# An fp32 encoder on one core: buffer rings and product order of the seven-product FFN tiles, a spread permutation, and the sums of the last norm

## The chip, the cores and the metric

The kernel runs on one core of a Trainium2 chip. A time is the device time of one execution in microseconds (us). TensorE is PE here (its weight loads are PEld), VectorE DVE, ScalarE ACT, GpSimd POOL, and SyncE, which only issues DMAs in this kernel, SP. A lower time is better.

## What is computed

The reference is a trunk of two encoder layers on 512 tokens of width 1024, in fp32. Each layer adds a token mixer, a cross-attention into a memory and a SwiGLU feed-forward part (FFN), each behind an RMS norm; a last RMS norm ends it. The change lies in the FFN and in the last norm:

```python
def rms_norm(x, g):
    y = x * lax.rsqrt(jnp.mean(x * x, axis=-1, keepdims=True) + EPS)
    return y * g

def swiglu(h, w_gate_up, w_down):
    g, u = jnp.split(h @ w_gate_up, 2, axis=-1)
    return (jax.nn.silu(g) * u) @ w_down

for i in range(2):
    x = x + mixer(rms_norm(x, g_mix[i]))
    x = x + memory_cross_attention(rms_norm(x, g_xq[i]), rms_norm(mem, g_mem[i]), ...)
    x = x + swiglu(rms_norm(x, g_ffn[i]), w_gate_up[i], w_down[i])   # 1024 -> 2 x 2816 -> 1024
return rms_norm(x, g_final)
```

## The kernel before

**Precision.** Every fp32 operand is split into a high part in PE's fast fp32 format (F32R) and a low part, the rest. A product is then three matmuls: high x high, high x low, low x high.

**FFN** (`ffn`, L1153). A layer has 22 gate/up tiles, each of 128 columns of gate and 128 of up. They come in rounds j = 0..7, 8..15 and 16..21, and behind each round stands a down stage that multiplies what the round made with the down weights and adds it to x. Tiles 0, 1, 20 and 21 are computed whole. The 18 between, j = 2..19, are seven-product tiles (`winograd`, L1122): the tile's product is taken as two by two blocks, and by Strassen's scheme in Winograd's form seven block products do for eight. `product` (L1112) issues one of them, 12 matmuls of 128 x 256 (line L1119), so a tile is 84 matmuls. A tile accumulates in three PSUM banks. The bank called mm takes A11, then A12 on top; S takes S2, then S3 and A22; T takes S1, then S4. `seven_tile` (L1196) and the u additions (L1130, L1135) and copies (L1128, L1132) put the parts together on DVE and ACT. A bank is reused by a tile two later; L1203 is the last to read S.

**Left factors** (`left_factors`, L1070). The 1 MB of weights of a tile arrives as a raw tile (ring of two, loaded by SP at L101 or L98). Three factors are plain blocks (A11, A12, A22, function `loaded`): ACT casts the high part (L1087), ACT writes the negated block, rounded to F32R, into the low half (L1088), and POOL issues a DMA of 256 KB that adds the block from HBM on top (L1089), which leaves the low part. Four factors are computed (S1, S2, S3, S4): DVE makes the sum (`summed`, L1095), ACT casts it (L1080), DVE subtracts (L1081). Each of the seven needs one buffer of 128 x 1024. `tile_of` takes them in turn from two rings of four, tagged wl and wh, in the order A11, S2, S1, A12, S3, S4, A22; seven being odd, a factor's ring changes from tile to tile.

**Order.** A scheduler places every engine's instructions in one order ahead of time, and gives a new tile the buffer of its ring that came free first. On the chip each engine then works through its list in that order and waits where an input or a buffer is missing. POOL's accumulate DMAs stand in POOL's list, raw loads in SP's.

**Permutation** (`by_columns`, L1146). The mixer of layer 1 wants the tokens in another order, so between rounds of layer 0 x is permuted: for each of its eight tiles an ACT copy (L1150) and a DVE copy back (L1151). It is called at j = 20 of layer 0.

**Last norm** (`last_step`, L1293). It works in two halves of 256 tokens, for m = 0..7: `sum_sq` (L138) squares x on ACT (L141) and adds into an accumulator on DVE or POOL (L145). At m = 7 `rstd_of` (L147) adds the last square on DVE (L148), sums over partitions by a matmul with ones (L152), scales (L135) and takes the power -1/2 on POOL (L136); ACT and DVE scale the result (L1315, L1317) and SP writes it (L1318).

Of the kernel before, what the change touches and what calls it, by code (L numbers as in the profile page):

```python
# [31 lines left out]
def trunk_kernel(  # L32
# [30 lines left out]
    def x_bank():  # L63
        return bank_of("X", 1)

    def o_bank():
        return bank_of("O", 1)

    def tmp():
        return pp.tile([P, 512], F32, tag="P", name="P")  # L70

    def small(n=4):
        return sm.tile([P, 8], F32, tag="sm", name="sm")[:, :n]
# [991 lines left out]
        T3, T4 = parts(tb)  # L1065
        return dict(T1=T1, T2=T2, T3=T3, T4=T4)

    turn = [0]

    def left_factors(v, src, room):  # L1070

        def tile_of():
            turn[0] ^= 1
            tag = ("wh", "wl")[turn[0]]
            hl = wp.tile([P, 1024], F32R, tag=tag, name=tag)
            return hl.rearrange("p (e k n) -> p e k n", e=2, k=4)

        def parts(x):
            hl = tile_of()
            nc.scalar.copy(hl[:, 0], x)  # L1080
            nc.vector.tensor_sub(hl[:, 1], x, hl[:, 0].bitcast(F32))  # L1081
            return hl[:, 0], hl[:, 1]

        def loaded(i):

            hl = tile_of()
            nc.scalar.copy(hl[:, 0], v[:, i])  # L1087
            nc.scalar.activation(hl[:, 1], v[:, i], AF.Copy, scale=-1.0)  # L1088
            nc.gpsimd.dma_start(hl[:, 1], src[:, i], accum_op=ALU.add)  # L1089
            return hl[:, 0], hl[:, 1]  # L1090

        def summed(op, x, y):
            t = room.tile([P, S], F32, tag="oT", bufs=8, name="ws")
            t = t.rearrange("p (k n) -> p k n", k=4)
            nc.vector.tensor_tensor(t, x, y, op=op)  # L1095
            return t
        r = {}
        a11, a12, a21, a22 = (v[:, i] for i in range(4))
        s1 = summed(ALU.add, a21, a22)
        r["A11"] = loaded(0)  # L1100
        s2 = summed(ALU.subtract, s1, a11)
        r["S2"] = parts(s2)
        r["S1"] = parts(s1)
        r["A12"] = loaded(1)
        s3 = summed(ALU.subtract, a11, a21)
        r["S3"] = parts(s3)
        s4 = summed(ALU.subtract, a12, s2)
        r["S4"] = parts(s4)
        r["A22"] = loaded(3)
        return r  # L1110

# [10 lines left out]
    def winograd(ph, A, Bs):  # L1122

        ba, bb, bd = (f()[:, :256] for f in (mm_bank, s_bank, t_bank))
        t = ph.tile([P, 4, 256], F32, tag="pth", bufs=2, name="pc")
        pc, u = t[:, 0:2], t[:, 2:4]
        product(ba, A, Bs, "A11", "B11", True)
        nc.scalar.copy(pc[:, 0], ba)  # L1128
        product(bb, A, Bs, "S2", "T2", True)
        nc.vector.tensor_add(u[:, 0], pc[:, 0], bb)  # L1130
        product(bd, A, Bs, "S1", "T1", True)
        nc.scalar.copy(pc[:, 1], bd)  # L1132
        product(ba, A, Bs, "A12", "B21", False)
        product(bb, A, Bs, "S3", "T3", False)
        nc.vector.tensor_add(u[:, 1], pc[:, 0], bb)  # L1135
        product(bd, A, Bs, "S4", "B22", False)
        product(bb, A, Bs, "A22", "T4", False)
        return ba, (u[:, 0], bd), (pc[:, 0], bb), (u[:, 1], pc[:, 1])
# [4 lines left out]
    def columns(t):  # L1143
        return t.rearrange("p (c r) -> p r c", r=8)

    def by_columns(ph):  # L1146

        for f in range(KF):
            t = ph.tile([P, S], F32, tag="oT", bufs=8, name="perm")
            nc.scalar.copy(columns(t), rows(xs[f]))  # L1150
            nc.vector.tensor_copy(xs[f], t)  # L1151

    def ffn(layer, ph, step, normed, fin):  # L1153
        wgu = w_gate_up[layer]
        wd = w_down[layer]
        lo, hi = slice(0, 256), slice(256, 512)
        whole = []

        def blocks(w):
            return w.rearrange("p e (k n) -> p e k n", k=4)  # L1160

        def whole_factors(j):

            v = load(wgu[j], 4, 4 * P).rearrange("p e (k n) -> p (e k) n", k=4)
            return [split(v[:, i * KF:(i + 1) * KF], KF, P) for i in range(2)]

        def factors(j):
            v = blocks(load(wgu[j], 4, 4 * P))
            return left_factors(v, blocks(wgu[j]), ph)

        cross(layer, ph, normed, lambda: whole.append(whole_factors(0)), step[0])
        xh, xl, Bs, rstd = step[1]()
        whole.append(whole_factors(1))
        bc = row_bcast(lambda: ph.tile([P, S], F32, tag="oT", bufs=8, name="bc"), rstd)

        def whole_tile(wg, wu, behind=None, own=0):


            bg, bu = s_bank(), t_bank()
            steps = [(b, w, i) for b, w in ((bg, wg), (bu, wu)) for i in range(KF)]  # L1180

            def issue(part):
                for bank, (wh, wl), i in part:
                    k = i % 2 * 4 + i // 2
                    mm3(bank, wh[:, k], wl[:, k], xh[i], xl[i], i == 0, i == KF - 1)
            if behind is None:
                issue(steps)
            else:
                issue(steps[:own])
                with tc.issue_after(behind):  # L1190
                    issue(steps[own:])
            g = ph.tile([P, S], F32, tag="ptl", bufs=2, name="g")
            nc.vector.tensor_mul(g, bg, bc)
            return g, bu

        def seven_tile(A):  # L1196
            c11, c12, c21, c22 = winograd(ph, A, Bs)
            g = ph.tile([P, 2, S], F32, tag="ptl", bufs=2, name="g")
            g, u = g[:, 0], g[:, 1]
            nc.vector.tensor_mul(g[:, lo], c11, bc[:, lo])  # L1200
            nc.vector.tensor_add(g[:, hi], *c12)
            nc.vector.tensor_mul(g[:, hi], g[:, hi], bc[:, hi])
            nc.vector.tensor_add(u[:, lo], *c21)  # L1203
            nc.vector.tensor_add(u[:, hi], *c22)
            return g, u

        A2 = None
        for f0, f1 in ((0, 8), (8, 16), (16, NF)):
            ah, al = [], []
            for j in range(f0, f1):  # L1210
                if layer == 0 and j == NF - 2:
                    by_columns(ph)
                if j == 0:
                    A2 = factors(2)
                if j < 2:
                    g, u = whole_tile(*whole[j], *((marks["sum"], 12) if j == 0 else (marks["bc"], 4)))
                elif j < NF - 2:
                    g, u = seven_tile(A2 if j == 2 else factors(j))
                else:
                    g, u = whole_tile(*whole_factors(j))  # L1220
                sg = tmp()
                nc.scalar.activation(sg, g, AF.Silu)
                nc.vector.tensor_mul(sg, sg, u)
                h = ph.tile([P, 2, S], F32R, tag="wo", bufs=8, name="act")
                h, l = h[:, 0], h[:, 1]
                nc.scalar.copy(h, sg)
                nc.vector.tensor_sub(l, sg, h.bitcast(F32))
                ah.append(h)
                al.append(l)
            n = f1 - f0  # L1230
            last = f1 == NF

            def down_weights(mp):
                return load(wd[f0 * P:f1 * P, mp * 256:(mp + 1) * 256].rearrange("(k p) n -> p k n", p=P), n, 256)

            if last and layer == 1:
                down_by_halves(down_weights, n, ah, al, bc, fin)
                break
            for mp in range(KF // 2):
                v = down_weights(mp)  # L1240
                for mj in range(2):
                    m = mp * 2 + mj
                    bank = down_bank(m)
                    wh, wl = split(v[:, :, mj * P:(mj + 1) * P], n, P)
                    for k in range(n):
                        mm3(bank, wh[:, k], wl[:, k], ah[k], al[k], k == 0, k == n - 1)
                    t = tmp()
                    if last:
                        nc.vector.tensor_mul(columns(t), rows(bank), rows(bc))
                    else:  # L1250
                        nc.vector.tensor_mul(t, bank, bc)  # L1251
                    (nc.vector if m % 2 or last else nc.gpsimd).tensor_add(xs[m], xs[m], t)  # L1252
                    if last:
                        fin(m)
# [38 lines left out]
    def last_step(ph, m, half):  # L1293
# [2 lines left out]
            nat.append(ph.tile([P, NT // 2, D], F32, tag="qT", bufs=2, name="nat"))  # L1296
            st["acc"] = tmp()[:, :256]
        xm = xs[m][:, half * 256:(half + 1) * 256]
        last = sum_sq(st["acc"], xm, m)
        xg = tmp()[:, :256]  # L1300
        nc.scalar.activation(xg, xm, AF.Copy, scale=gcols[:, 67 + m:68 + m])
        b = (t_bank() if m % 2 else s_bank())[:, :256]
# [2 lines left out]
        nc.vector.tensor_copy(nat[half][:, :, m * P:(m + 1) * P],  # L1305
                              b.rearrange("p (t d) -> p t d", t=2))
        if m == KF - 1:
            rstd = rstd_of(st["acc"], last, nc.vector)
            for t in range(2):
                n = nat[half][:, t]  # L1310
                w = D // 2
# [90 lines left out]
```

## Time and profile before

| | |
|---|---|
| median of three runs | 1389.03 us (1387.33 to 1391.44) |
| the profiled execution | 1391.77 us, span 1390.0 us |
| mean granted clock of PE | 0.993 of full speed |
| PE busy | 1346.9 us (97%) |
| DVE busy | 988.7 us (71%) |
| ACT busy | 791.7 us (57%) |
| POOL busy | 446.8 us (32%) |

The span runs from the first instruction to the last; times in the trace count from its start. An engine's busy time says how much it has to do, not where it holds the others up. For that one looks at what PE waited for, at the chain of work that ended last, and at the windows in which a wait falls. Durations below are those of the one profiled execution, which lies 2.7 us above the median.

### The profile page before, as it was taken

Reading aid. Unit: us, or ns where it says so; the run is one execution under the profiler, and the core shown is the slowest. Engines: PE = TensorE matmul, PEld = TensorE weight load, DVE = VectorE, ACT = ScalarE, POOL = GpSimd, SP = SyncE. Lnnn points to the kernel's source line nnn. Section 1 sums busy time; section 2 is a strip of 40 time slices with the busy share of each in tenths; the row PEclk is TensorE's granted clock in tenths of the full one; section 3 lists DMA queues with packets and bytes.
Section 4 is the critical chain, followed back from the end, with each engine's and each line's share of the span. In section 5 each row is a group of like instructions: output and inputs, shape, how many; then the busy total and the mean of one; then the engine's idle time right before and its main releaser. Section 6 shows DMA issues by size and latency. Waiting matters only on the chain.

```text
span 1390.0 us, 24186 instructions
## 1 busy us (share of the span) xinstructions
PE 1346.9 (97%) x9131; PEld 1231.2 (89%) x9131; DVE 988.7 (71%) x1950; ACT 791.7 (57%) x1601; POOL 446.8 (32%) x575
## 2 busy tenths in 40 slices
PE   8898999999999999999999999999999999999997
PEld 8897889998998998898987888798989989998996
DVE  6988886778865875676579745657697766856765
ACT  5467775656743663473468555655566626743543
POOL 4856445212212220200324546842122112212111
PEclk9999999999999999999999999999999999999999
DMA  7111023312853873553122132134207636754721
GB/s 238 62 61 31 1 92 122 122 62 39 191 151 100 189 186 112 135 145 95 50 71 67 33 91 85 61 110 144 82 9 167 175 106 156 175 140 115 181 69 61
DMA packets 93086, 148.78 MB, mean 107 GB/s; under 512 B 7520, under 2 KB 65835, under 8 KB 87339
## 3 DMA queue, kind: packets, MB, share of 16 engines
q1 hardware_dynamic: 77418, 118.93, 26.6%
q0 software_dynamic: 15552, 28.32, 12.4%
q8 instruction: 72, 1.18, 0.3%
q14 instruction: 44, 0.35, 0.1%
HBM read 145.13 MB, written 2.10 MB: 106 GB/s over the span
## 4 chain that ended last, share of the span: by engine, by line
PE 77%; DVE 8%; DMA 7%; ACT 4%; issue 3%; POOL 1%; SPq 0%; POOLq 0%; ACTq 0%; DVEq 0%
PE mm L129 12%; PE mm L130 12%; PE mm L131 12%; PE S L1119 8%; PE mm L1119 6%; PE T L1119 5%; DMA wl<-in_w_gate_up_dram 3%; PE O L553 2%; PE S L129 2%; PE S L130 2%; PE S L131 2%; PE T L275 2%; PE T L130 1%; PE T L129 1%; PE T L131 1%
## 5 line engine op out<-in xcount | busy, mean ns | idle before, releaser
L117 ACT CAST wh<-raw 128x1024 fp32r<-128x1024 f32 (+4 forms) x132 | 130.3, 991 | 139.4 <-PE mm L130 50.9
L123 DVE TENSOR_TENSOR wl<-raw,wh 128x1024 fp32r<-128x1024 f32 (+3 forms) x114 | 139.1, 1221 | 25.8 <-ACT wh L117 23.7
L256 POOL TENSOR_SCALAR P<-P,sm 128x512 f32<-128x512 f32 (+2 forms) x128 | 80.7, 643 | 82.1 <-DVE sm L254 62.6
L1089 POOL DMA_DIRECT2D wh<-in_w_gate_up_dram x54 | 47.0, 871 | 166.2 <-ACT wh L1088 103.4
L130 PE MATMUL mm<-act,wh 128*128 128x512 f32 (+1 forms) x264 | 98.9, 375 | 0.0
L131 PE MATMUL mm<-act,wl 128*128 128x512 f32 (+1 forms) x264 | 98.7, 375 | 0.0
L129 PE MATMUL mm<-act,wh 128*128 128x512 f32 (+1 forms) x264 | 98.3, 376 | 0.0
L1119 PE MATMUL S<-bf,wl 128*128 128x256 f32 x648 | 87.2, 283 | 1.1 <-DVE pc L1135 1.1
L1119 PE MATMUL S<-bf,wh 128*128 128x256 f32 x648 | 86.2, 283 | 0.0
L1089 POOL DMA_DIRECT2D wl<-in_w_gate_up_dram x54 | 47.3, 876 | 114.1 <-ACT wl L1088 42.8
L1119 PEld LDWEIGHTS S<-bf,wl 128*128 128x128 f32 x648 | 81.8, 192 | 1.5 <-DVE pc L1135 1.5
L1119 PEld LDWEIGHTS S<-bf,wh 128*128 128x128 f32 x648 | 81.9, 192 | 0.5
L1095 DVE TENSOR_TENSOR ws<-raw 128x512 f32<-128x512 f32 x72 | 49.5, 688 | 40.4 <-DMA raw<-in_w_gate_up_dram 40.4
L129 PE MATMUL mm<-wh,xgh 128*128 128x256 f32 (+1 forms) x256 | 74.1, 290 | 3.0 <-ACT rt L418 2.3
L145 POOL TENSOR_TENSOR P<-P 128x512 f32<-128x512 f32 (+1 forms) x21 | 26.4, 1255 | 152.8 <-ACT P L141 152.8
L1252 POOL TENSOR_TENSOR x<-x,P 128x512 f32<-128x512 f32 x16 | 25.2, 1577 | 153.5 <-DVE P L1251 153.5
L1080 ACT CAST wh<-ws 128x512 fp32r<-128x512 f32 x72 | 44.5, 619 | 50.2 <-PE mm L130 17.7
L131 PE MATMUL mm<-wh,xgl 128*128 128x256 f32 (+1 forms) x256 | 73.1, 286 | 0.0
L130 PE MATMUL mm<-wl,xgh 128*128 128x256 f32 (+1 forms) x256 | 73.1, 286 | 0.0
L123 POOL TENSOR_TENSOR wl<-raw,wh 128x256 fp32r<-128x256 f32 x80 | 59.1, 770 | 31.6 <-ACT wh L117 31.6
L279 DVE TENSOR_TENSOR ptl<-T,pth 128x512 fp32r<-128x512 f32 (+2 forms) x96 | 57.6, 616 | 13.3 <-ACT pth L278 13.1
L1087 ACT CAST wh<-raw 128x512 fp32r<-128x512 f32 x54 | 33.6, 621 | 54.7 <-PE mm L130 23.6
(420 smaller groups left out, 4758.4 us busy)
## 6 DMA issues: line engine op xcount, KB each, us to landing
raw<-in_w_gate_up_dram SPq DMA_DIRECT2D x44, 1024.0 KB, 5.5
raw<-in_w_down_dram SPq DMA_DIRECT2D x16, 1024.0 KB, 5.6
wl<-in_w_gate_up_dram POOLq DMA_DIRECT2D x54, 256.0 KB, 5.7
wh<-in_w_gate_up_dram POOLq DMA_DIRECT2D x54, 256.0 KB, 5.7
raw<-in_w_xkv_dram SPq DMA_DIRECT2D x8, 1024.0 KB, 5.2
raw<-in_w_down_dram SPq DMA_DIRECT2D x8, 768.0 KB, 4.9
raw<-in_w_in_ab_dram SPq DMA_DIRECT2D x5, 1024.0 KB, 6.7
raw<-in_w_out_ab_dram SPq DMA_DIRECT2D x4, 1024.0 KB, 5.1
```

Of the source, the lines that this page charges most:

```text
L117: nc.scalar.copy(hv, v)
L123: low.tensor_sub(lv[:, q], v[:, q], hv[:, q].bitcast(F32))
L129: nc.tensor.matmul(o, lh, rh, start=start, stop=False)
L130: nc.tensor.matmul(o, lh, rl, start=False, stop=False)
L131: nc.tensor.matmul(o, ll, rh, start=False, stop=stop)
L256: nc.gpsimd.tensor_scalar(p, p, ri[:, j:j + 1], 1.0, op0=ALU.mult, op1=ALU.mult)
L279: nc.vector.tensor_sub(ptl[:, k0:k1, j * P:(j + 1) * P], tv, hv.bitcast(F32))
L1080: nc.scalar.copy(hl[:, 0], x)
L1087: nc.scalar.copy(hl[:, 0], v[:, i])
L1089: nc.gpsimd.dma_start(hl[:, 1], src[:, i], accum_op=ALU.add)
L1095: nc.vector.tensor_tensor(t, x, y, op=op)
L1119: nc.tensor.matmul(bank, x, y, start=start and k == 0 and i == 0, stop=k == n - 1 and i == 2, skip_group_check=True)
```

## The change

Four edits. First, the rings: a loaded factor always takes a buffer of the ring wl, a computed one always one of wh (three and four a tile). Second, in `winograd` the product S2 is issued ahead of A11. Third, the permutation is called in four pieces of two tiles, at j = 16 to 19. Fourth, in the last norm the squares of m = 6 and m = 7 are not added to the accumulator on DVE or POOL; accumulator and squares go to PE each by itself, as matmuls with ones that add up in PSUM (six of one column in each half, where two were).

```diff
     def left_factors(v, src, room):
-        def tile_of():
-            turn[0] ^= 1
-            tag = ("wh", "wl")[turn[0]]
+        def tile_of(tag):
             hl = wp.tile([P, 1024], F32R, tag=tag, name=tag)
...
         def parts(x):
-            hl = tile_of()
+            hl = tile_of("wh")
...
         def loaded(i):
-            hl = tile_of()
+            hl = tile_of("wl")
...
+        product(bb, A, Bs, "S2", "T2", True)
         product(ba, A, Bs, "A11", "B11", True)
         nc.scalar.copy(pc[:, 0], ba)
-        product(bb, A, Bs, "S2", "T2", True)
...
-    def by_columns(ph):
+    def by_columns(ph, fs):
-        for f in range(KF):
+        for f in fs:
...
-                if layer == 0 and j == NF - 2:
-                    by_columns(ph)
+                if layer == 0 and 16 <= j < 20:
+                    by_columns(ph, (2 * j - 32, 2 * j - 31))
...
-        last = sum_sq(st["acc"], xm, m)
+        if m < KF - 2:
+            sum_sq(st["acc"], xm, m)
+        else:
+            sq = tmp()[:, :256]
+            nc.scalar.activation(sq, xm, AF.Square)
+            if m == KF - 2:
+                st["sums"] = x_bank()[:, 0:1], o_bank()[:, 0:1]
+            for a in (st["acc"], sq) if m == KF - 2 else (sq,):
+                for t in range(2):
+                    nc.tensor.matmul(st["sums"][t], a[:, t * P:(t + 1) * P], ones[:, 0:1],
+                                     start=a is st["acc"], stop=m == KF - 1)
...
-            rstd = rstd_of(st["acc"], last, nc.vector)
+            rstd = small(2)
+            mean = small(2)
+            for t in range(2):
+                nc.vector.tensor_scalar(mean[:, t:t + 1], st["sums"][t], 1.0 / D, EPS, op0=ALU.mult, op1=ALU.add)
+            nc.gpsimd.tensor_tensor(rstd, mean, mhalf[:, :2], op=ALU.pow)
```

In the changed kernel lines have moved up by four in most of the FFN: the matmuls of a product are L1115, the casts and subtractions of computed factors L1076 and L1077, of loaded ones L1083 and L1084, the accumulate L1085, the sums L1091, the u additions L1126 and L1131, the last reader of S L1199, the permutation L1146 and L1147.

**PE, j = 11 to 12 in layer 0.** Before, from S3 of one tile (12 matmuls into S) to the second matmul of the next tile's A11 (bank mm):

```order
L1119 MATMUL S<-bf,wh 128x256 x12
L1119 MATMUL mm<-xgh,wl 128x256
L1119 MATMUL T<-xgh,wl 128x256
L1119 MATMUL T<-xgl,wl 128x256
L1119 MATMUL T<-xgh,wl 128x256 x2
L1119 MATMUL T<-xgl,wl 128x256
L1119 MATMUL T<-xgh,wl 128x256 x2
L1119 MATMUL T<-xgl,wl 128x256
L1119 MATMUL T<-xgh,wl 128x256 x2
L1119 MATMUL T<-xgl,wl 128x256
L1119 MATMUL T<-xgh,wl 128x256
L1119 MATMUL mm<-xgl,wl 128x256
```

With the change, from the same S3 on:

```order
L1115 MATMUL S<-bf,wh 128x256 x14
L1115 MATMUL T<-xgh,wh 128x256
L1115 MATMUL T<-xgl,wh 128x256
L1115 MATMUL T<-xgh,wh 128x256 x2
L1115 MATMUL T<-xgl,wh 128x256
L1115 MATMUL T<-xgh,wh 128x256 x2
L1115 MATMUL T<-xgl,wh 128x256
L1115 MATMUL T<-xgh,wh 128x256 x2
L1115 MATMUL T<-xgl,wh 128x256
L1115 MATMUL T<-xgh,wh 128x256
L1115 MATMUL S<-bf,wh 128x256 x10
L1115 MATMUL mm<-xgh,wl 128x256
```

Before, the first A11 matmul stood ahead of S4 (into T) and the rest right behind it; now two matmuls of S2 stand there (they make 14 of the first row), its other ten behind S4, and A11 after them.

**ACT, the start of round two in layer 0.** The numbers of raw name the tile: 5537 is the round's first seven-product tile (A11 5541, A12 5553, S4 5564 and A22 5567), 5675 its second (A11 5679). Before:

```order
L1080 CAST wh_5564<-ws_5562 128x512
L1080 CAST wl_5559<-ws_5557 128x512
L1087 CAST wh_5679<-raw_5675 128x512
L1088 ACTIVATE wh_5679<-raw_5675 128x512
L1087 CAST wl_5567<-raw_5537 128x512
L1088 ACTIVATE wl_5567<-raw_5537 128x512
L1128 COPY pc_5574<-mm_5571 128x256
```

With the change:

```order
L1083 CAST wl_5567<-raw_5537 128x512
L1084 ACTIVATE wl_5567<-raw_5537 128x512
L1076 CAST wh_5564<-ws_5562 128x512
L1083 CAST wl_5679<-raw_5675 128x512
L1084 ACTIVATE wl_5679<-raw_5675 128x512
L1076 CAST wh_5685<-ws_5683 128x512
L1125 COPY pc_5574<-mm_5571 128x256
```

The first tile's A22 (from raw_5537) stood behind the second tile's A11; now it stands ahead of it, and so does the cast of S4.

**DVE, j = 4 and 5 in layer 0.** g_4709 belongs to the tile j = 3 and its last addition reads the bank S_4618; ws_4999 is the first sum of the tile j = 6 and waits for its raw load. Before:

```order
L1081 TENSOR_TENSOR wl_4869<-ws_4867,wl_4869 128x512
L1130 TENSOR_TENSOR pc_4758<-pc_4758,S_4756 128x256
L1202 TENSOR_TENSOR g_4709<-g_4709,bc_4327 128x256
L1203 TENSOR_TENSOR g_4709<-pc_4620,S_4618 128x256
L1095 TENSOR_TENSOR ws_4999<-raw_4997 128x512
L1223 TENSOR_TENSOR P_4715<-P_4715,g_4709 128x512
L1081 TENSOR_TENSOR wh_4872<-ws_4861,wh_4872 128x512
```

With the change:

```order
L1198 TENSOR_TENSOR g_4709<-g_4709,bc_4327 128x256
L1223 TENSOR_TENSOR act_4580<-P_4577,act_4580 128x512
L1077 TENSOR_TENSOR wh_4748<-ws_4746,wh_4748 128x512
L1077 TENSOR_TENSOR wh_4869<-ws_4867,wh_4869 128x512
L1091 TENSOR_TENSOR ws_4999<-raw_4997 128x512
L1199 TENSOR_TENSOR g_4709<-pc_4620,S_4618 128x256
L1091 TENSOR_TENSOR ws_5005<-ws_4999,raw_4997 128x512
```

The addition that frees the S bank stood ahead of the sum that waits for the load; now it stands right behind it.

## Rows read from the trace of the kernel before

**Rows 1.** The page of the profiled execution, part 1.

```profile
PE 1346.9 (97%) x9131; PEld 1231.2 (89%) x9131; DVE 988.7 (71%) x1950; ACT 791.7 (57%) x1601; POOL 446.8 (32%) x575
```

**Rows 2.** The table by windows, busy us summed over six FFN stretches of 340 us.

```profile
sum 340.00, PE 332.93 PEld 325.39 DVE 261.83 ACT 227.07 POOL 79.19; mean PE 55.49 PEld 54.23 DVE 43.64 ACT 37.85 POOL 13.20
```

**Rows 3.** Waits of PE (total, times, longest): layer 0, layer 1; one on the timeline.

```profile
PE mm L1119 <- ACT pc L1128: 1.2, 1, 1.2
PE S L1119 <- DVE pc L1135: 1.1, 1, 1.1
PE mm L1119 <- DMA wl<-in_w_gate_up_dram: 0.8, 1, 0.8
...
PE mm L1119 <- DMA wl<-in_w_gate_up_dram: 3.0, 4, 1.7
PE mm L1119 <- DMA wh<-in_w_gate_up_dram: 0.8, 2, 0.4
...
1065.48 0.50 PE L1119 MATMUL mm<-xgh,wl 128*128 128x256 f32 x2 [1.70 <-DMA wl<-in_w_gate_up_dram]
```

**Rows 4.** The chain that ended last, from 350 to 583 us: start, length, what.

```profile
350.47 2.89 PE S L1119 x24
...
446.95 7.94 DMA raw<-in_w_gate_up_dram
...
573.16 8.94 DMA raw<-in_w_gate_up_dram
```

**Rows 5.** The timeline of ACT, then of POOL, from 477 to 479 us.

```profile
477.24 0.62 ACT L1087 CAST wl<-raw 128x512 fp32r<-128x512 f32 x1 [0.30 <-PE S L1119]
...
478.69 0.87 POOL L1089 DMA_DIRECT2D wl<-in_w_gate_up_dram  x1 [1.48 <-DVE pc L1130]
```

**Rows 6.** The accumulate line L1089: one alone (503 us), then all of layer 1.

```profile
DMA to landing us min/median/max: 4.0/4.0/4.0
...
DMA to landing us min/median/max: 4.0/5.7/9.0
```

**Rows 7.** The tile of the permutation: its copies on ACT and on DVE.

```profile
L1150 ACT COPY perm<-x x8: 1165/1210/1217, 590.2 to 602.9; 128x512 f32<-128x512 f32 x8
L1151 DVE COPY x<-perm x8: 420/427/428, 593.2 to 604.2; 128x512 f32<-128x512 f32 x8
```

**Rows 8.** Line L1089 at 446, 572, 1152 and 1278 us: one accumulate each.

```profile
DMA to landing us min/median/max: 6.8/6.8/6.8
...
DMA to landing us min/median/max: 6.1/6.1/6.1
...
DMA to landing us min/median/max: 8.0/8.0/8.0
...
DMA to landing us min/median/max: 6.0/6.0/6.0
```

**Rows 9.** A wait of DVE in layer 1 (total, times, longest); then its timeline.

```profile
DVE ws L1095 <- DMA raw<-in_w_gate_up_dram: 21.0, 15, 2.3
...
492.93 0.69 DVE L1095 TENSOR_TENSOR ws<-raw 128x512 f32<-128x512 f32 x1
```

**Rows 10.** The tile of the raw loads: 455-520 us, 1287-1300 us.

```profile
DMA to landing us min/median/max: 5.3/5.6/5.8
...
DMA to landing us min/median/max: 5.2/6.2/7.3
```

**Rows 11.** The timeline of the end; then L152 in the first half.

```profile
1379.85 0.42 ACT L141 ACTIVATE P<-x 128x256 f32<-128x256 f32 x1 [1.39 <-DVE x L1286]
1380.36 0.43 DVE L148 TENSOR_TENSOR P<-P 128x256 f32<-128x256 f32 x1 [0.28 <-ACT P L141]
1380.71 0.44 PE L1304 MATMUL T<-identr,P 128*128 128x128 f32 x2 [1.65 <-ACT P L1301]
1380.88 0.53 PEld L152 LDWEIGHTS X<-ones,P 128*128 128x128 f32 x4
...
L152 PE MATMUL X<-ones,P x4: 169/250/250, 1364.0 to 1364.2; 128*128 128x1 f32 x4
```

More of the change, by code (lines that the diff above doesn't have):

```diff
@@ L1066, in right_factors @@
         return dict(T1=T1, T2=T2, T3=T3, T4=T4)
-    turn = [0]
     def left_factors(v, src, room):
-        def tile_of():
-            turn[0] ^= 1
-            tag = ("wh", "wl")[turn[0]]
+        def tile_of(tag):
             hl = wp.tile([P, 1024], F32R, tag=tag, name=tag)
```

## The prediction

> **What bounds the kernel now.** I read the page first, then the table by windows, then the waits, then the chain and the timeline around each wait. The page [rows 1] is to show that TensorE (PE) is busy in 97% of the span: what the change can give back is PE idle time. The windows [rows 2] are to show how much of it lies in the change's reach: in six stretches of seven-product tiles PE is busy for 332.93 of 340 us and lacks 7.07. DVE is busy for 262 us there, so it has less room than ACT with 227. The waits [rows 3] name nine gaps: seven end with the landing of an accumulate DMA (the low part of an A11 factor), one with L1135 on DVE, one with the ACT copy L1128.
>
> These idle times are too short as they stand. A matmul record lasts 0.283 us, yet the next one starts 0.120 us later (24 in 2.88 us, [rows 4]), so each gap is really 0.16 us longer; and the second matmul after a gap starts 0.10 late as well (two take 0.50, [rows 3], not 0.28 + 0.12). The nine waits sum to 6.9 us, and 9 x 0.26 makes it 9.25. At five more places the gap is too small for the view; from the starts of the matmuls I estimate 1.25 us there. Together **10.5 us**: A11 waits 7.4, two waits behind a raw load 1.6, the permutation 1.4.
>
> How each arises. A11: after the last matmul that reads a ring buffer, ACT casts and negates and POOL issues; 477.24 to 478.69 is 1.45 us [rows 5], and with the handover 1.61 from the release. The DMA then lands after 4.0 us at best, 5.7 in the median and up to 9.0 [rows 6], so release to landing is 5.6 to 10.6. Today A11 at most tiles takes a buffer that was freed 55 to 64 matmuls of 0.12 us (6.6 to 7.7 us) before its low part is read. Raw: DVE stands in order; the sum L1095 waits for a 1 MB load of 7.94 or 8.94 us, [rows 4], and L1135, on which PE depends, stands behind it. Permutation: eight ACT copies of 1.21 us at 590 to 603 us [rows 7], and L1128 at 607.7 is behind them.
>
> **The change part by part.**
>
> *Rings.* The same 18 x 3 accumulates and 18 x 4 computed factors run in each layer: nothing is added on any engine. What moves is which buffer each takes, and by the order on PE I counted the matmuls from release to low read. For A11 it becomes 60 to 74 (7.2 to 8.9 us) at most tiles, the product order included. A12 has 98 or more, A22 114 or more. The A22 of a round's first tile finds its buffer free some 6 us earlier, and ACT, and POOL's queue after it, take that A22 ahead of the second tile's A11 instead of behind it. SP's queue keeps its order, and the raw load that waits there for this A22's casts goes earlier too; with that the two waits of L1135 go (-1.6). **But at the second tile of rounds two and three of each layer it falls**, from 9.1 us to 52 matmuls, 6.24 us: there PE still starts A11 ahead of S2, and ACT does S4's cast ahead of A11's. The time needed is 1.61 + 0.52 for that cast, plus the DMA. That DMA is not in the trace, so I bound it: from below by the lone one, 4.0 us [rows 6] (wait 0), from above by the same four tiles today, whose DMAs run beside raw loads and took 6.8, 6.1, 8.0 and 6.0 us [rows 8]: 1.61 + those, less 6.24, makes 2.2 + 1.5 + 3.4 + 1.4 = 8.4 us for the four. Since A22's DMA, which today runs beside it, will be out of the way by some 6 us, I take the low end, 4.0 to 4.7 us: 0.4 a tile, **1.6 us**.
>
> The row says that a lone 256 KB accumulate takes 4.0 us [rows 6]. The Trainium skill, page "DMA: Bandwidth & Descriptors", section "Anatomy of one DMA — SWDGE (gpsimd) path", fits a GpSimd-issued DMA as 2.0 us plus bytes over 436 GB/s, an estimated 2.6 us here. By that figure the four tiles would not wait at all and the sum would be 1.6 us lower; the trace speaks against it, and I use the row.
>
> *S2 first.* S2 needs no DMA, only cast and subtraction, and its T2 right factor is ready. What it needs sooner is the S bank and its two sums: S2 now starts 1.8 us after A22 of two tiles before ends at the least, where it was 3.0. In that time DVE must do L1203, which frees the bank (an addition of that size takes 0.43, [rows 11]). At ten tiles that row now stands behind the s1 sum of the next raw load, or the u0 addition does. Walking the order with 0.69 us a sum [rows 9] and a raw load of 5.5 us, the bank is free 0.68 us early at six tiles, the addition 0.95 early at four. Raw loads in mid-stage took 5.3 to 5.8, in the third round up to 7.3 [rows 10], so a few of them run over by some tenths: I put **0.7 us** between 0 and the second rival's price.
>
> *The other A11s.* 7.2 to 8.9 us against a chain of 1.61 + 5.7 in the median [rows 6]: some still run late. Bounds are 0 and today's 7.4; with a tile's three DMAs now spread over one ring I take **0.7**.
>
> *Permutation.* Four of the ACT copies go into the down stage ahead of round three, four into its first tiles. The same 8 x 1.21 us of ACT and 8 x 0.43 of DVE run where PE has weights ready and no pc copy stands behind; -1.4. If this cover were missing, the wait would come back at most once, 1.4.
> Today's DVE copies at 593 to 604 run beside accumulates, and no PE wait in [rows 3] ends with one of those DMAs. The Trainium skill, page "SBUF — State Buffer", section "SBUF: two separate sides", holds that an fp32 SBUF copy on DVE keeps GpSimd from writing descriptors. By it the four copies beside the first tile's DMAs would cost at most 4 x 0.43 = 1.7 us; the rows show no such wait, and I take nothing.
>
> *Tail.* After the last Square (ends 1380.27) DVE's L148 took 0.43 and with its handover held PE until 1380.88 [rows 11]. Now two small matmuls follow the Square: -0.6; the second tensor_scalar gives 0.15 back: -0.45. The extra matmuls are four per half, two passes each, a pass 0.08 us [rows 11] to 0.12 us [rows 4] after the last; I take 0.11. In the second half PE idles for 1.65 us there [rows 11] and they are covered; in the first half PE is the bound, +0.9. Net **+0.45**, between -0.45 and +0.9.
>
> *Sum*: -10.5 + 1.6 + 0.7 + 0.7 + 0.45 = -7.05. The profiled execution took 1391.8 us, 2.7 above the median of the runs; its waits are taken as those of any run, so the median becomes 1389.0 - 7.05 = **1382.0 us**.
>
> **The rivals.**
> *(a) At four tiles the change does not do what it says*: A11 still comes first there, with the shortest distance of all, and its DMA stays as slow as today: +8.4 instead of 1.6, sum -0.25, 1388.8 us. For it: rows 8 are measured there. Against: A22's DMA moves away.
> *(b) DVE's order* (slower): at ten tiles the S bank or u0 waits behind a sum that waits for a raw load. If raw loads took 7.9 us as at 446.95 [rows 4], six waits of 1.7 and four of 1.5 cost 16.2 us where I put 0.7: 1382.0 + 15.5 = 1397.5. The gain is used up from a load of 7.1 us on. For it: DVE already waits 21.0 us for raw loads in one FFN [rows 9]. Against: mid-stage loads stay at 5.3 to 5.8 [rows 10].
> *(c) The DMAs crowd*: three accumulates through one ring come at other moments, and the A11 waits stay at 7.4 (for 1.6 + 0.7): 1387.1 us.
>
> **How the numbers follow.** My forecast has 0.70, each rival 0.10. About 0.3%, 4.2 us, is what a measurement can tell from no change: 1384.8 and 1393.2 are the marks. My own range is 1378 (every rest at zero) to 1386; a tenth of its 0.70 lies above 1384.8, and a fifth of (a) and (c) stops short of their price and stays faster: 0.63 + 0.04 = 0.67. Slower is (b) less its mild end, 0.08. The rest, 0.25, is within 0.3%. The range runs from 1378.5 to 1389.0, which takes in (a) and (c) and leaves out (b).
>
> **What would show it.** Right: on the timeline of the changed kernel no wait of L1115 for wl at third and later tiles of a round; short ones at the second tiles of rounds two and three; none for a pc copy near 607. L1091's waits for raw stay near 20 us a layer and none of PE's waits ends with L1199 or L1126. Wrong: PE waits of over 1 us for wl at the four second tiles (a), for DVE's L1199 or L1126 with a raw load ahead (b), or for wl spread over all tiles (c). In the tail the first L1317 should start some 0.5 us after the last Square's matmuls begin, with no DVE addition between.

## The result

The change is slower: 1398.19 us in the median (1395.15 to 1401.62, five runs) beside 1389.03 us, a ratio of 1.0062 (95% interval 1.0046 to 1.0079). The forecast was 1382.0 us; the second rival, DVE's order, had 1397.5.

The page of the changed kernel, its first lines. PE has 6 us more of busy time than in [rows 1] and the span is 9.8 us longer.

```profile
span 1399.8 us, 24105 instructions
...
PE 1353.0 (97%) x9147; PEld 1239.8 (89%) x9147; DVE 982.8 (70%) x1950; ACT 792.7 (57%) x1601; POOL 444.6 (32%) x573
```

The waits of PE in the changed kernel (total, times, longest), first in the FFN of layer 0, then of layer 1. These are all that the view has for the seven-product matmuls, L1115.

```profile
PE S L1115 <- DVE g L1199: 5.9, 3, 2.5
...
PE S L1115 <- DVE g L1199: 8.1, 3, 3.1
```

Of the nine waits of [rows 3] none is left: no A11, no pc copy, no u1. In their place stand six, all for L1199, the addition that frees the S bank, and together they are 14.0 us long where the nine had 6.9. The wait of the raw sums, which [rows 9] gave with 21.0 us in layer 1, has grown to 33.1 us:

```profile
DVE ws L1091 <- DMA raw<-in_w_gate_up_dram: 33.1, 16, 4.7
```

One of the six, on the timeline of the changed kernel: POOL's accumulates (A11, A12, A22 of one tile), SP's raw load, then DVE, then PE.

```profile
483.56 0.86 POOL L1085 DMA_DIRECT2D wl<-in_w_gate_up_dram  x1 [3.60 <-ACT wl L1084]
485.21 0.86 POOL L1085 DMA_DIRECT2D wl<-in_w_gate_up_dram  x1 [0.79 <-ACT pc L1128]
487.61 0.86 POOL L1085 DMA_DIRECT2D wl<-in_w_gate_up_dram  x1 [1.54 <-PE S L1115]
...
487.34 0.33 SPq L101 DMA_DIRECT2D raw<-in_w_gate_up_dram  x1
...
496.45 0.69 DVE L1091 TENSOR_TENSOR ws<-raw 128x512 f32<-128x512 f32 x1 [4.21 <-DMA raw<-in_w_gate_up_dram]
497.06 0.41 DVE L1199 TENSOR_TENSOR g<-pc,S 128x256 f32<-128x256 f32 x1
...
497.53 0.80 PE L1115 MATMUL S<-bf,wh 128*128 128x256 f32 x2 [2.53 <-DVE g L1199]
```

The three accumulates are issued within 4.1 us, and the raw load goes out 2.1 us behind the second of them and 0.3 us ahead of the third. It lands 9.1 us later, at 496.4. DVE's list has the first sum of that load (L1091) ahead of L1199, so L1199 starts at 497.06, though the A22 matmuls that it reads had ended over 4 us before; PE, which needs the bank for S2, stands for 2.53 us. One tile earlier DVE has the same two instructions in the same order, but the load, issued at 478.82, took 5.3 us, and PE did not wait:

```profile
DMA to landing us min/median/max: 5.3/5.3/5.3
...
484.14 0.69 DVE L1091 TENSOR_TENSOR ws<-raw 128x512 f32<-128x512 f32 x1 [0.94 <-DMA raw<-in_w_gate_up_dram]
484.75 0.41 DVE L1199 TENSOR_TENSOR g<-pc,S 128x256 f32<-128x256 f32 x1
```

In the whole kernel the first sum of a raw load stands directly ahead of L1199 at ten of the 36 tiles. At six of them the load took 7.9 to 9.7 us, and these are the six waits; at the other four it took 5.3 to 5.5 us, and PE had none.

In the kernel before, at the tile of the 2.53 us wait, POOL's and SP's timeline read:

```profile
481.92 0.86 POOL L1089 DMA_DIRECT2D wh<-in_w_gate_up_dram  x1 [2.36 <-ACT wh L1088]
486.06 0.86 POOL L1089 DMA_DIRECT2D wl<-in_w_gate_up_dram  x1 [3.28 <-ACT wl L1088]
...
485.79 0.33 SPq L101 DMA_DIRECT2D raw<-in_w_gate_up_dram  x1
```

There A12 went out 3.9 us ahead of the load, A22 0.3 us behind it, and the load took 5.3 us. Over the second rounds of the two layers (455 to 520 us, 1160 to 1225 us) the raw loads of the changed kernel landed after

```profile
DMA to landing us min/median/max: 5.3/6.9/9.2
...
DMA to landing us min/median/max: 5.3/7.2/9.7
```

where the kernel before had 5.6 in the median and at most 5.8 us from 455 to 520 [rows 10], and 5.6 and 7.6 from 1160 to 1225. Loads of down weights that start in these windows are among them.

Behind a wait PE is slow as well. The table by windows around 497 us: window, its length, busy us of the engines, then PEclk, the clock that was granted.

```profile
core 0: us, PE busy (x) PEld busy (x) DVE busy (x) ACT busy (x) POOL busy (x), PEclk, DMA share, GB/s
492.70:494.70 2.00, 2.00 (x19) 2.00 (x18) 0.00 (x0) 2.00 (x5) 0.73 (x1) 1.00 0.63 157
494.70:497.50 2.80, 0.30 (x3) 0.10 (x1) 1.05 (x3) 1.06 (x3) 0.99 (x2) 0.94 0.68 117
497.50:500.00 2.50, 2.47 (x11) 2.47 (x12) 2.50 (x5) 0.62 (x1) 0.00 (x0) 0.50 0.68 116
500.00:502.00 2.00, 2.00 (x17) 2.00 (x16) 2.00 (x4) 0.62 (x1) 0.00 (x0) 0.85 0.01 1
502.00:504.00 2.00, 2.00 (x19) 2.00 (x18) 0.60 (x3) 1.31 (x3) 0.51 (x1) 1.00 0.03 8
```

The granted clock falls to 0.50, the lower of its two levels (1.2 GHz), when PE starts again after the wait, and is back at 1.00 by 502 us; 11 matmuls ran in 2.5 us where 19 run in 2.0. It fell so behind four of the six waits (those of 2.02, 2.53, 3.10 and 2.34 us), not behind the other two (1.35 and 2.63 us). Between the starts of one seven-product matmul and the next, what goes beyond the usual 0.12 us adds up to 21.3 us in the changed kernel, 15.4 us of it at the waits and 5.9 us elsewhere, nearly all of that matmuls at the slow clock, and to 10.6 us in the kernel before. The difference, 10.7 us, is close to what the profiled executions differ by (9.85 us; the medians by 9.2).

The other two edits did what they were to do. The permutation's copies now run between 550 and 588 us, and PE has no wait for a pc copy:

```profile
L1146 ACT COPY perm<-x x8: 1140/1180/1206, 550.1 to 587.4; 128x512 f32<-128x512 f32 x8
```

In the last norm, on the timeline of the end, the last Square, the first sum, the first tensor_scalar, the power and the scaling:

```profile
1390.26 0.42 ACT L1299 ACTIVATE P<-x 128x256 f32<-128x256 f32 x1 [1.39 <-DVE x L1282]
1390.73 0.38 PE L1304 MATMUL X<-ones,P 128*128 128x1 f32 x2 [0.40 <-ACT P L1299]
1391.15 0.16 DVE L1317 TENSOR_SCALAR sm<-X 128x1 f32<-128x1 f32 x1 [0.36 <-PE X L1304]
1391.61 0.71 POOL L1318 TENSOR_TENSOR sm<-sm,mhalf 128x2 f32<-128x2 f32 x1 [7.30 <-DVE sm L1317]
1392.35 1.33 ACT L1325 ACTIVATE nat<-nat,sm 128x512 f32<-128x512 f32 x2 [1.27 <-POOL sm L1318]
```

From the start of the last Square to the first sum it is 0.47 us, where [rows 11] had 1.03 (1379.85 to 1380.88). From the last matmul of the last down stage to the end of the span it is 11.08 us, where it was 11.66. But the stretch ahead of that, from the last 512-column matmul, which stands ahead of both halves of the last down stage, has grown from 38.20 to 38.77 us; PE does six of the one-column matmuls for the first half in it, where it did two. Together it is 49.85 us in both kernels.

### The profile page after: what moved, and what is told of

The parts are those of the page before. It is cut to its first block, busy times and chain, and to the rows that moved or that the text cites. A ratio compares the mean times of both kernels' runs of the same rounds, so it can differ in the third digit from the quotient of the medians.

```text
span 1399.8 us, 24105 instructions
## 1 busy us (share of the span) xinstructions
PE 1353.0 (97%) x9147; PEld 1239.8 (89%) x9147; DVE 982.8 (70%) x1950; ACT 792.7 (57%) x1601; POOL 444.6 (32%) x573
## 4 chain that ended last, share of the span: by engine, by line
PE 83%; DVE 6%; DMA 5%; ACT 3%; issue 2%; POOL 0%; SPq 0%; POOLq 0%; ACTq 0%; DVEq 0%
PE mm L129 12%; PE mm L130 12%; PE mm L131 12%; PE S L1115 10%; PE mm L1115 7%; PE T L1115 6%; DMA raw<-in_w_gate_up_dram 4%; PE O L553 3%; PE S L129 2%; PE S L130 2%; PE S L131 2%; PE T L275 2%; PE T L130 1%; PE T L131 1%; PE T L129 1%
## 5 line engine op out<-in xcount | busy, mean ns | idle before, releaser
L1085 POOL DMA_DIRECT2D wl<-in_w_gate_up_dram x108 | 94.0, 870 | 280.6 <-ACT wl L1084 154.7
L1076 ACT CAST wh<-ws 128x512 fp32r<-128x512 f32 x144 | 87.8, 621 | 97.4 <-PE S L1115 31.2
L1115 PE MATMUL S<-bf,wh 128*128 128x256 f32 x864 | 122.0, 291 | 14.0 <-DVE g L1199 14.0
L1115 PEld LDWEIGHTS S<-bf,wh 128*128 128x128 f32 x864 | 113.9, 198 | 15.6 <-DVE g L1199 15.2
L1115 PE MATMUL mm<-xgh,wl 128*128 128x256 f32 x576 | 118.0, 286 | 0.0
L1077 DVE TENSOR_TENSOR wh<-ws,wh 128x512 fp32r<-128x512 f32 x144 | 97.9, 685 | 0.7
L1115 PEld LDWEIGHTS mm<-xgh,wl 128*128 128x128 f32 x576 | 96.3, 195 | 0.2 <-DMA wl<-in_w_gate_up_dram 0.2
L1091 DVE TENSOR_TENSOR ws<-raw 128x512 f32<-128x512 f32 x72 | 49.5, 688 | 60.9 <-DMA raw<-in_w_gate_up_dram 60.9
L1115 PE MATMUL mm<-xgl,wl 128*128 128x256 f32 x288 | 82.0, 285 | 0.0
L1083 ACT CAST wl<-raw 128x512 fp32r<-128x512 f32 x108 | 66.8, 619 | 23.0 <-PE mm L1115 16.6
```

The source lines that it names most:

```text
L1115: nc.tensor.matmul(bank, x, y, start=start and k == 0 and i == 0, stop=k == n - 1 and i == 2, skip_group_check=True)
```

## The experiments

Three theories stood against each other. **R**: the ring split brings three accumulates and a raw load together, the load becomes long, and DVE's order hands this on to the S bank. **S**: S2 first costs by itself, since it needs the bank sooner. **C**: the clock fell, for whatever reason, and that is the loss. All kernels of a group ran on one chip with the kernel before; each interval is that of the ratio to it.

### One part alone, one part undone

The ring split alone (A11 first, permutation and last norm as before):

```diff
-        def tile_of():
+        def tile_of(tag):
...
-            hl = tile_of()
+            hl = tile_of("wh")
...
-            hl = tile_of()
+            hl = tile_of("wl")
```

> The kernel before with the ring split alone (loaded factors in wl, computed ones in wh; A11 still the first product, permutation and last norm as before). Three theories. R: the ring split lets the three accumulates of every second tile start within 4 us, beside one raw load, which then takes 8 to 9.7 us instead of 5.5, and it places the first sum of that load on DVE ahead of the addition that frees the S bank. S: S2 first is what costs, because it needs the S bank 1.4 us sooner, whatever the rings. C: PE's granted clock fell (0.988 in the changed kernel), and that is the loss. Here R expects raw loads of 8 us and more again where accumulates bunch, and PE waits for DVE of 5 to 15 us in all behind the raw sum, by the order's slack of 0.7 to 1.5 us at some 20 tiles: 1388 to 1400 us. S expects no wait for the S bank and the A11 waits reduced: 1383 to 1387. C makes no difference between the edits and expects the clock to tell: 1395 or more with a clock of 0.99 or less.

Measured: 1386.99 us beside 1387.55, ratio 0.9993 (0.9982 to 1.0004). Waits of PE for L1199, layer 0 and layer 1:

```profile
PE S L1115 <- DVE g L1199: 2.0, 2, 1.4
...
PE S L1115 <- DVE g L1199: 1.5, 1, 1.5
```

So the bank waits come with A11 first too, three of them and 3.5 us, less than R's 5 to 15, and A11 waits of 1.9 us are left; the split gains nothing that can be told from zero. The time lies just under R's range and in that of S, but S expected no such wait. Theory C's 1395 us did not come. The ring split also sets DVE's order: in the traces the first sum of a raw load stands at most three instructions ahead of the addition that frees the S bank at 18 of the 36 tiles here and at 12 in the change, and at none in the kernel before and in the runs with the rings in turn.

S2 first alone, rings in turn:

```diff
+        product(bb, A, Bs, "S2", "T2", True)
         product(ba, A, Bs, "A11", "B11", True)
         nc.scalar.copy(pc[:, 0], ba)
-        product(bb, A, Bs, "S2", "T2", True)
```

> The kernel before with S2 issued ahead of A11 alone; rings in turn as before. R expects raw loads of 5.2 to 6.5 us in the middle of the rounds, no PE wait for the addition that frees the S bank, and A11 waits only at the second tiles of rounds two and three (A11 has 8.8 to 11.2 us elsewhere, 6.5 there): some 2 us left of 7.4, so 1382 to 1385 us. S expects the six waits of 1.5 to 3.3 us for the S bank as in the change, 1393 to 1397. C expects no gain unless the clock rises.

Measured: 1393.69 us, ratio 1.0039 (1.0025 to 1.0053). The time lies in S's range, but none of S's waits came: there is no wait for the S bank. The raw loads are as R said (the second rounds, as above), and R's time is missed:

```profile
DMA to landing us min/median/max: 5.7/5.9/6.2
...
DMA to landing us min/median/max: 5.6/5.8/5.9
```

A11 waits are left, 6.7 us in all (layer 0, layer 1), and the longest, four of 1.2 to 2.8 us by the matmuls' starts (452, 581, 1157 and 1283 us), are at the second tiles of rounds two and three:

```profile
PE mm L1119 <- DMA wh<-in_w_gate_up_dram: 4.1, 3, 2.6
...
PE mm L1119 <- DMA wh<-in_w_gate_up_dram: 2.6, 3, 1.3
```

That is my rival (a): A11 is early and close behind its buffer's release at just these four tiles, and its DMA runs beside a raw load. In the change, with the rings split, it did not come. Three waits of 1.9 us in all for ACT's cast L1080, which the kernel before does not have, and the permutation's wait stand beside these.

The change without its ring split was slower than the kernel before too:

```diff
-        def tile_of(tag):
+        def tile_of():
+            turn[0] ^= 1
+            tag = ("wh", "wl")[turn[0]]
```

> The change with its ring split undone (S2 first, permutation spread and sums on PE stay). R expects what S2 first alone gives, with the permutation's wait of 1.4 us gone and 0.5 us more on the path in the last norm: 1381 to 1384 us, and no wait of L1128 behind the permutation. S expects the change's time, 1396 to 1399.

Measured: 1392.35 us, ratio 1.0032 (1.0016 to 1.0048); A11 waits of 3.5 and 3.0 us in the two layers, none behind the permutation, none for the S bank. Its twelve executions lie in two bunches, six of 1388.3 to 1390.6 us and six of 1394.1 to 1396.7; the profile is one of the lower, and what parts them no run shows. R's number is missed, by the profile for the same reason as in the run before; S is out, for S2 first stands here without its waits.

The permutation and the last norm alone (the change with its ring split undone, as above, and A11 as the first product again):

> The kernel before with the spread permutation and the last norm's sums on PE alone; rings in turn, A11 first. My terms were -1.4 for the permutation and +0.45 for the last norm: 1386 to 1389 us, no wait of L1119 for a pc copy near 607 us, the A11 and raw waits as before (9 us in all), and in the tail no DVE addition ahead of the sums. If the permutation's copies on DVE delay the accumulates that run beside them, an A11 wait near 575 to 600 us grows by up to 1.7 us instead.

Measured: 1389.16 us beside 1389.67, ratio 0.9997 (0.9984 to 1.001). No wait behind the permutation is left; the A11 and raw waits are 7.5 us in the view of this one profile, where [rows 3] have 5.7 without the pc copy. The two edits are worth nothing that can be told from zero.

### Where the chain is cut

One edge more in the change: on DVE the first sum of a raw load goes behind the addition that frees the S bank of three tiles before.

```diff
-            nc.vector.tensor_add(u[:, lo], *c21)
+            marks["g"] = marks.get("g", []) + [nc.vector.tensor_add(u[:, lo], *c21).ins]
...
-        s1 = summed(ALU.add, a21, a22)
+        if len(marks.get("g", ())) > 2:
+            with tc.issue_after(marks["g"][-3]):
+                s1 = summed(ALU.add, a21, a22)
+        else:
+            s1 = summed(ALU.add, a21, a22)
```

> The change with one ordering edge more: on DVE the first sum of a raw load stands behind the addition that frees the S bank of three tiles before. Nothing else. R expects the raw loads as long as in the change (8 to 9.7 us at every second tile) but the six PE waits for the bank gone, 15 us and what the clock lost behind them: 1380 to 1384 us. If the late loads instead hold up the computed factors themselves, PE waits for S2's halves at the same tiles and 1388 to 1395 remain. C expects 1395 or more with a clock of 0.99 or less, since the clock would not depend on these waits.

Measured: 1383.77 us, ratio 0.9972 (0.9955 to 0.9988); again in a later group 1382.57 us, ratio 0.9954 (0.994 to 0.9969). The raw loads are as long as in the change (the second rounds again), and the timeline of DVE shows the addition start 2.5 us ahead of the late load's sum:

```profile
DMA to landing us min/median/max: 5.5/8.2/9.1
...
DMA to landing us min/median/max: 5.5/8.5/9.8
```

```profile
498.91 0.42 DVE L1203 TENSOR_TENSOR g<-pc,S 128x256 f32<-128x256 f32 x1 [0.68 <-PE S L1119]
501.40 0.69 DVE L1091 TENSOR_TENSOR ws<-raw 128x512 f32<-128x512 f32 x1 [2.08 <-DMA raw<-in_w_gate_up_dram]
```

The waits of PE that are left in the FFN are 1.5 us in the view:

```profile
PE S L1119 <- DVE pc L1130: 0.8, 1, 0.8
PE mm L1119 <- DMA wl<-in_w_gate_up_dram: 0.3, 1, 0.3
...
PE S L1119 <- DVE pc L1135: 0.4, 2, 0.2
```

The late load by itself costs PE next to nothing; it cost because L1199 stood behind it. The clock's falls in the FFN went with the waits, while the mean granted clock of this profile is 0.992, no higher than the 0.993 of the kernel before; so C falls.

The other end of the chain, the change with one accumulate fewer:

```diff
-            nc.gpsimd.dma_start(hl[:, 1], src[:, i], accum_op=ALU.add)
+            if i != 1:
+                nc.gpsimd.dma_start(hl[:, 1], src[:, i], accum_op=ALU.add)
```

> The change without the accumulate DMA of A12 (two accumulates a tile instead of three; the low part of A12 is then only the negated high part, so the output is not the reference's). DVE's order is the change's, with the sum of a raw load ahead of the addition that frees the S bank. Theory R (bunched accumulates lengthen the load): in the change and in the run with one edge more, a raw load whose last accumulate ahead of it was issued 1 to 3.4 us earlier took 8.1 and 8.5 us in the median, one with 3.4 us or more 5.2 to 5.8; that neighbour is A12's. So the raw loads of the middle of a round fall to 5.2 to 6.3 us, the six waits for the S bank to under 0.5 us each, the clock dips behind them go, and the time is 1379 to 1384 us. Rival R2 (a raw load is long at every second tile for another reason, such as its own issue moment beside A22's accumulate): the loads stay at 8 us and more, the waits stay, 1394 to 1398.

Measured: 1379.64 us, ratio 0.9928 (0.9913 to 0.9943). DVE's order is the change's, and PE has no wait in the FFN that the view shows. The raw loads of the second rounds:

```profile
DMA to landing us min/median/max: 5.3/5.5/5.6
...
DMA to landing us min/median/max: 5.2/5.3/5.6
```

So the neighbour that stretches the load is A12's accumulate; R2 falls. By the age of the last accumulate issued ahead of a load into the raw ring (gate/up or down weights) that starts beside A22's: in the kernel before 28 loads with 3.4 to 5 us had a median of 5.6 us, in the change 18 with 1 to 3.4 us had 8.1, in the run with the edge 26 such had 8.5, and without A12's accumulate the 32 that start beside A22's all lie between 5.2 and 6.2 us.

### Is S2 first needed, and the change beside its mended forms

The run with the edge, but A11 first:

> The change with the ordering edge (raw sum behind the addition that frees the S bank), but A11 as the first product. It tells whether S2 first adds anything once DVE's order is mended. By the order A11 has 6.0 to 8.9 us from release to low read as with the ring split alone, where A11 waits of 1.9 us were seen in all: I expect A11 waits of 2 to 4 us, none for the S bank, 1384 to 1387 us. If S2 first is worth nothing: 1382 to 1385, as the run with the edge. If S2 first is what mends the A11 waits wholly: 1386 to 1389.

Measured: 1383.0 us, ratio 0.9955 (0.9937 to 0.9973), within the intervals of the two runs with S2 first. S2 first adds nothing that can be seen here. I had expected A11 waits and the view shows none. My reason was the order of the split alone; in the order that was built here A11 has, as I count it, 7.4 to 8.9 us from release to low read at all but the four second tiles, since the edge moves the matmuls too. No row of the trace shows that distance itself.

The ring split and the edge, nothing else (the diffs above):

> The ring split and the ordering edge alone: A11 first, permutation and last norm as in the kernel before. If the split is a gain as soon as DVE's order does not pass a late raw load on to the S bank, the waits of the ring split alone for the addition that frees the bank (3.5 us) go, and with them what its u0 waits and clock cost: 1383 to 1386 us beside 1387.0 for the split alone; the permutation's wait near 607 us stays (1.4). If the edge only works together with S2 first, it stays at 1386 to 1389.

Measured: 1380.18 us, ratio 0.9941 (0.9919 to 0.9963). The waits for the S bank are gone; three A11 waits are left (layer 0, layer 1), in a profile of the longest of the six executions, 1385.9 us:

```profile
PE mm L1119 <- DMA wl<-in_w_gate_up_dram: 1.7, 2, 1.3
...
PE mm L1119 <- DMA wl<-in_w_gate_up_dram: 1.4, 1, 1.4
```

The permutation's wait, which I expected to stay, is not in the view, nor in that of the split alone: with the rings split it is gone without the spread.

The change once more on the same chip:

> The change once more, unaltered, on the chip of the other two runs of this group, so that the three stand beside each other: 1395 to 1400 us, six waits of PE for the addition that frees the S bank, each behind a raw load of 7.9 us or more, and a granted clock near half behind the longer of them.

Measured: 1398.34 us, ratio 1.0059 (1.0037 to 1.0081), with six waits for L1199 of 11.3 us in all (layer 0, layer 1):

```profile
PE S L1115 <- DVE g L1199: 4.3, 3, 2.5
...
PE S L1115 <- DVE g L1199: 7.0, 3, 2.9
```

The granted clock fell behind three of them. Against it stands, in the same group,

> The change with the ordering edge, once more beside the change: 1381 to 1385 us, 13 to 17 us below it, if the six waits and the clock behind them are the whole of what the change lost.

with its 1382.57 us: one edge takes 15.8 us off. The table sets the time that PE lost in the two FFNs (starts of seven-product matmuls beyond 0.12 us apart, from one profile each) beside the medians. The groups ran on different chips, and the kernel before had 1387.6, 1389.7 and 1389.0 us in the three.

| kernel | median us | PE time lost in the FFNs, us |
|---|---|---|
| before (first group) | 1389.0 | 10.6 |
| the change | 1398.2 | 21.3 |
| the change again | 1398.3 | 19.2 |
| ring split alone | 1387.0 | 10.6 |
| S2 first alone | 1393.7 | 14.8 |
| change without ring split | 1392.4 | 11.3 |
| permutation and last norm alone | 1389.2 | 11.3 |
| change and edge | 1383.8 | 3.3 |
| change and edge, again | 1382.6 | 3.1 |
| change and edge, A11 first | 1383.0 | 1.3 |
| ring split and edge | 1380.2 | 3.9 |
| change without A12's accumulate | 1379.6 | 0.4 |

From before to the change 10.7 us more lost give 9.2 us more time; within the last group, from the change to the edge, 16.1 less give 15.8 less. Single medians stand up to 4 us off that line; each profile is one execution.

## Why the prediction was wrong

*Bound and places.* Right: the time to win or lose was PE's waits in the seven-product tiles, and the nine waits behind the 10.5 us that were read from [rows 3 to 4] were all removed.

*Rings.* Right, and better than forecast: no A11 wait in the one profile and one of 0.6 us in the other, where I left 1.6 + 0.7, and the waits of L1135 gone. That includes the second tiles, where I argued that A22's DMA would be out of the way. The runs with S2 first and the rings in turn have the waits of rival (a) there. The upper bound for these four tiles, 8.4 us, left out the 0.52 us of the cast that the same paragraph counts; with it, it is 10.5.

*S2 first: the step that failed.* I put 0.7 us on it; the waits cost 15.4 us, and with the clock 21.3. The mechanism was worked out: the raw sum ahead of L1203, 0.68 us to spare at a load of 5.5 us. What was wrong is the load. I took its time from [rows 10], the kernel before, as if it were the load's own. It belongs to what runs beside it, and the same paragraph on the rings moved exactly that: three accumulates into one ring. I walked A11's times through the changed order, but not those of A12 and A22; in the trace of the change the last accumulate ahead is 1.2 to 2.9 us old at 14 of the 24 gate/up loads that start beside A22's. And [rows 4] held two loads of 7.94 and 8.94 us, with an accumulate issued 0.8 us ahead of each; I used them as the rival's price and not as a warning. The kernel before has six loads of that kind, and all six took 7.4 to 8.9 us.

The rival had the mechanism and a break-even at 7.1 us, against loads of 7.9 to 9.7 at the six waits; its chance of 0.10 was too low. That its numbers fit so well (16.2 us of waits priced and 15.4 measured, 1397.5 us forecast and 1398.2 measured) is in part luck: it priced ten waits of 1.5 to 1.7 us, four of them for u0, and six of 1.4 to 3.1 us came, none for u0 in this profile; and neither it nor the sum had a term for the clock, which took up to 5.9 us.

The title of that step misled as well: S2 first by itself does not make these waits. Three of them come with A11 first, and none comes with the rings in turn; DVE's order behind them is the split's too. With S2 first beside it they are twice as many and four times as long in all. By the order S2 first takes 1.4 us of slack more, and of the 32 loads that start beside A22's accumulate 14 have another one 1 to 2.5 us ahead in the change, 2 in the split alone. How much each of the two adds no run parts.

*The other terms.* Permutation -1.4: no wait is left, but as the split alone removes it too, the spread cannot be credited with it in the change. Last norm +0.45: from the last 512-column matmul to the end the four profiles with the old sums show 49.6 to 50.1 us and the eight with the new ones 49.8 to 50.3, so it is too small to tell from zero; the end gave back 0.58 us where I had 0.45, and the first half cost 0.57 where I had 0.9. The Trainium skill's price for a GpSimd-issued DMA, on the page "DMA: Bandwidth & Descriptors", section "Anatomy of one DMA — SWDGE (gpsimd) path", was set aside for the lone 4.0 us; between 480 and 500 us of the changed kernel accumulates took 4.3 to 9.1 us, so the trace speaks against it here too. The Trainium skill's page "SBUF — State Buffer", section "SBUF: two separate sides", would have had the DVE copies hold up POOL's descriptors. In the run with the permutation and the last norm alone an accumulate issued at 587.3 us, between two of the copies, took 4.7 us; the kernel before has 4.8 at that place without copies.

## What to carry to other kernels

A transfer's time in a trace is the time beside its neighbours of that trace: when a change moves when other transfers are issued, price it again from the rows where such neighbours do stand beside it, however few. Look along each in-order engine for a short instruction that others wait for and that stands behind one that waits for a transfer; with one ordering edge it can go first, and then the late transfer costs nothing. Splitting rings by what fills them is a gain here only with that edge: ring split and edge alone ran 8.8 us below the kernel before.

## What the runs showed of the hardware that was not expected

A 1 MB load of SP's queue took 5.2 to 6.2 us beside a single 256 KB accumulate of POOL's queue that started with it (32 loads, without A12's accumulate), and 5.3 to 9.8 us when another had been issued 1 to 3.4 us ahead (medians 8.1 and 8.5 us, 44 loads of two kernels). Within 1 to 2.5 us ahead it was 6.6 to 9.8 us at all 31 of them, 8.7 in the median of either kernel. In these runs the transfer that came later bore it: with S2 first alone the next A11 was issued 1.3 to 1.7 us behind the load, at 21 of 22 places the load took 5.6 to 6.2 us, and that accumulate took 6.5 to 8.1 us, where a lone one takes 4.0 [rows 6].

The granted clock fell to half behind waits of PE of 2.02, 2.34, 2.53 and 3.10 us in stretches that were otherwise full, and stayed there for 3.4 us; behind one of 2.63 us it did not fall. In the second profile of the change it fell behind waits of 1.98, 2.12 and 2.51 us and not behind one of 2.85, so the length of the wait alone does not decide it. A fall cost about 1.5 us more (5.9 us at four), and the sum of the waits alone understates the loss by 5.9 of 21.3 us.
